# Router fed from x1, one route for the last four tiles, and a first expert's list built by one-hot matmuls

## The chip, the cores and the metric

The kernel runs on one core of a Trainium2 chip. The metric is the device time of one execution in microseconds, as the median of several runs. TensorE (PE) multiplies matrices, VectorE (DVE), ScalarE (ACT) and GpSimd (POOL) work on tiles of 128 partitions, SyncE (SP) issues most DMAs, and sixteen DMA engines move the data. The five engines run their own instruction streams in program order and wait for each other on semaphores.

## The reference

One layer of a mixer block on x of 2048 tokens by 1024 features (conditioning vector `c`), then a mixture of experts with 32 experts in 4 groups of 8. What bears on this change is its second half:

```python
mix = jnp.concatenate([y_conv, y_att, y_pool], axis=-1) @ w_out[l]
x = x + g1 * mix
h = _rmsnorm(x, norm2_g[l]) * (1 + sc2) + sh2
x = x + g2 * _hier_moe(h, ...)          # then a final rmsnorm
# in _hier_moe, per token (hf = h):
g_prob = softmax(hf @ rg_w + rg_b);           g_p, g_idx = top_k(g_prob, 1)
e_logits = einsum('td,dge->tge', hf, re_w) + re_b
e_sel = e_logits of group g_idx;              e_p, e_idx = top_k(softmax(e_sel), 2)
gates = g_p * e_p / sum(e_p)
y = (silu(hb @ w1[e]) * (hb @ w3[e])) @ w2[e]  # per expert e, hb = its tokens
out[token] += gate * y
```

Everything is float32. Each token goes to two experts of one group; expert weights are 1024 by 512 (w1, w3) and 512 by 1024 (w2).

## The kernel before

Convolution, projections and attention fill the span up to about 1144 us. The change lies in the two stages behind them.

**Output stage**, `output()` (L1087). It takes 16 tiles of 128 tokens. For a tile, `product` multiplies with w_out; `mm3` makes each float32 product of three passes on float32r parts (lines L92, L93, L94: high by high, low by high, high by low), so 48 matmuls of 512 columns. Then x1 = x + g1\*mix (L1132, L1133), a sum of squares on ACT (L1136), and h2 = x1\*s\*A2 + B2 on DVE (L1138, L1139), where s is 1/rms. h2 is written to memory (L1140, profile name h_d). `router` (L1142) transposes h2 on PE (L1152), copies it from PSUM on ACT (L1153), multiplies with the 36 router columns `rw` (L1157) and adds the bias (L1159). When a group of tiles (`GROUPS`: 4, 4, 4, 2, 2) has its logits, `route` (L1278) picks group and experts with a chain of small DVE instructions (L1269 to L1337), counts on PE how many earlier tokens each expert has (L1312 to L1318), and POOL scatters the entries (token, gate) into the experts' lists in memory, `list_d`, two indirect DMAs per tile (L1340). At the end `order` (L1344) ranks the experts by their counts into `ordi`.

**Experts**, `moe()` (L1420). The first two experts are fixed (`FIRST`), the other 30 come in the order of `ordi`, one SP register load each (L1451, TENSOR_LOAD). For an expert, SP reads its list (`gather`, L1573: `ent` from `list_d`), POOL gathers the tokens' rows (L1575: `xg` from `h_d`), PE transposes them (`flip`, L1603), and PE multiplies with the weights by `mm3`. The weights (`wr`, 512 KB or 1 MB loads, SP L1641) are cut into high parts on ACT (`wh`, L1657) and low parts on DVE or POOL (`wl`, L1658). Results are scattered back with L1708.

The order of instructions on every engine is set by a scheduler that works from estimated costs; the Python order and `issue_after` only bound it. An instruction that waits holds all behind it on its engine.

Of the kernel before, what the change touches and what calls it, by code (L numbers as in the profile page):

```python
# [10 lines left out]
F32 = mybir.dt.float32  # L11
# [3 lines left out]
I32 = mybir.dt.int32  # L15
AF = mybir.ActivationFunctionType
OP = mybir.AluOpType
# [4 lines left out]
T = 2048  # L22
D = 1024
# [24 lines left out]
class K:  # L48
# [1040 lines left out]
    def output(self):  # L1089
# [6 lines left out]
        with ExitStack() as c1:  # L1096
# [7 lines left out]
            with tc.issue_after(self.last.ins):  # L1104
# [5 lines left out]
                self.row(A2, 2)  # L1110
                rw = wp.tile([128, KT, 36], F32, name="rw")
# [4 lines left out]
                nc.sync.dma_start(rb[:, 4:36], a["router_e_b"].rearrange("o g e -> o (g e)").to_broadcast([128, 32]))  # L1116
            lgs = {}
            where = [(c, i) for c, n in enumerate(self.GROUPS) for i in range(n)]

            def product(t, mix):  # L1120
# [5 lines left out]
                for k in range(KT):  # L1126
                    for m in range(2):
                        s = slice(m * 512, (m + 1) * 512)
                        self.mm3(ps[:, m, :], mh[:, k, ti], ml[:, k, ti], W[k][0][:, s], W[k][1][:, s],
                                 k == 0, k == KT - 1)  # L1130
                h2 = st.tile([128, D], F32, name="h2", tag="h2", bufs=3)
                nc.vector.tensor_tensor(h2, ps.rearrange("p a b -> p (a b)"), g1, OP.mult)  # L1132
                nc.vector.tensor_tensor(x, x, h2, OP.add)  # L1133
                (nc.scalar if t == NT - 1 else nc.sync).dma_start(self.x1_d[t * 128:(t + 1) * 128], x)
                s = st.tile([128, 3], F32, name="s2", tag="s2", bufs=4)
                nc.scalar.activation(h2, x, AF.Square, accum_out=s[:, 0:1])  # L1136
                self.rsqrt(s[:, 2:3], s[:, 0:1], D, s[:, 1:2])
                nc.vector.scalar_tensor_tensor(h2, x, s[:, 2:3], A2, op0=OP.mult, op1=OP.mult)  # L1138
                nc.vector.tensor_tensor(h2, h2, B2, OP.add)  # L1139
                (nc.scalar if t == NT - 1 else nc.sync).dma_start(self.h2_d[t * 128:(t + 1) * 128], h2)  # L1140
                return h2

            def router(t, h2):
# [15 lines left out]
                nc.vector.tensor_tensor(lgs[c][:, i, :], pr[:, :36], rb, OP.add)  # L1159
# [67 lines left out]
    def route_consts(self, wp):  # L1227
# [31 lines left out]
        nc.vector.tensor_copy(self.capi, self.capr)  # L1259
# [566 lines left out]
```

## Time and profile before

| | |
|---|---|
| median of 3 runs | 2230.25 us (2230.12 to 2230.81) |
| profiled execution | 2232.48 us, of which the span 2230.6 us |
| PE busy in the span | 2008.2 us (90%) |
| DVE, ACT, POOL busy | 71%, 54%, 39% |
| DMA traffic | 569.64 MB, mean 255 GB/s |

In the profile, L numbers are lines of the kernel before; an arrow reads "output <- input". `big` and `sm` are PSUM tiles, `W` and `S`, `R`, `L` hold cut parts of w_out, `mh` and `ml` the high and low parts of the mixed input. A name in square brackets with a time is the idle time of the engine just before, and what ended it. PE is busy nearly without a break in the output stage and in most of the experts; between them, from 1362 to 1407 us, it is mostly idle.

### The profile page before, as it was taken

Reading aid. Unit: us, or ns where it says so; the run is one execution under the profiler, and the core shown is the slowest. Engines: PE = TensorE matmul, PEld = TensorE weight load, DVE = VectorE, ACT = ScalarE, POOL = GpSimd, SP = SyncE. Lnnn points to the kernel's source line nnn. Section 1 sums busy time; section 2 is a strip of 40 time slices with the busy share of each in tenths; the row PEclk is TensorE's granted clock in tenths of the full one; section 3 lists DMA queues with packets and bytes.
Section 4 is the critical chain, followed back from the end, with each engine's and each line's share of the span. In section 5 each row is a group of like instructions: output and inputs, shape, how many; then the busy total and the mean of one; then the engine's idle time right before and its main releaser. Section 6 shows DMA issues by size and latency. Waiting matters only on the chain. (4 is left out here: it accounts for less than half of the span.)

```text
span 2230.6 us, 37562 instructions
## 1 busy us (share of the span) xinstructions
PE 2008.2 (90%) x12823; PEld 1508.2 (68%) x12824; DVE 1578.8 (71%) x3007; ACT 1214.8 (54%) x2026; POOL 868.6 (39%) x1592
## 2 busy tenths in 40 slices
PE   5899999988889999988889995799999999999983
PEld 4777886855667777767767884557776666666762
DVE  5696899668878888886445555657766766766673
ACT  4832323256778887777642222546665665665552
POOL 4542112546454333365000113234544445554443
PEclk9999999998999999999999997899999999999987
DMA  8737978869977666668867436699999899999884
GB/s 283 259 120 231 277 219 278 292 188 295 293 236 224 200 206 197 206 190 276 225 220 277 152 124 224 237 291 358 336 316 319 279 347 319 338 326 313 304 297 141
DMA packets 312468, 569.64 MB, mean 255 GB/s; under 512 B 34547, under 2 KB 147656, under 8 KB 311240
## 3 DMA queue, kind: packets, MB, share of 16 engines
q1 hardware_dynamic: 287496, 489.26, 66.7%
q0 software_dynamic: 22304, 68.41, 10.7%
q10 hardware_dynamic: 2464, 9.44, 1.1%
q8 instruction: 105, 1.72, 0.3%
q14 instruction: 99, 0.81, 0.1%
HBM read 462.44 MB, written 103.53 MB: 254 GB/s over the span
## 5 line engine op out<-in xcount | busy, mean ns | idle before, releaser
L1658 DVE TENSOR_TENSOR wl<-wr,wh 128x1024 fp32r<-128x1024 f32 x314 | 393.1, 1289 | 173.0 <-ACT wh L1657 172.6
L1657 ACT ACTIVATE wh<-wr 128x1024 fp32r<-128x1024 f32 x372 | 374.2, 1053 | 243.7 <-PE acc L94 172.4
L93 PE MATMUL acc<-wl,xh 128*128 128x512 f32 (+3 forms) x544 | 219.4, 404 | 7.5 <-DVE wl L1658 3.9
L1026 DVE CUSTOM_DVE_ANT_0 L<-pl,bias 128x512 f32<-128x512 f32 (+3 forms) x312 | 180.3, 607 | 62.2 <-PE pt L1064 35.9
L92 PE MATMUL acc<-wh,xh 128*128 128x512 f32 (+3 forms) x544 | 217.0, 409 | 5.6 <-ACT wh L1657 5.2
L94 PE MATMUL acc<-wh,xl 128*128 128x512 f32 (+3 forms) x544 | 216.5, 401 | 0.0
L1025 PE MATMUL pl<-kc,qa 128*128 128x512 f32 (+3 forms) x640 | 183.6, 393 | 17.0 <-DMA kc<-kh_d 9.8
L863 DVE SCALAR_TENSOR_TENSOR S<-rel,wi,S 128x512 f32<-128x512 f32 (+3 forms) x259 | 171.2, 683 | 33.2 <-ACT rel L862 32.7
L1066 ACT ACTIVATE pT<-pt 128x512 f32<-128x512 f32 (+1 forms) x288 | 159.2, 577 | 63.9 <-PE pt L1064 62.9
L1064 PE MATMUL pt<-identr,L 128*128 128x128 f32 x1088 | 172.0, 284 | 20.5 <-ACT pT L1066 14.2
L1658 POOL TENSOR_TENSOR wl<-wr,wh 128x1024 fp32r<-128x1024 f32 x58 | 145.0, 2560 | 95.7 <-ACT wh L1657 92.5
L862 ACT ACTIVATE rel<-pi 128x512 f32<-128x512 f32 (+3 forms) x296 | 154.4, 549 | 48.1 <-PE pi L860 29.3
L627 DVE SCALAR_TENSOR_TENSOR ac<-u,kc,ac 128x512 f32<-128x512 f32 x240 | 175.0, 769 | 0.1
L1064 PEld LDWEIGHTS pt<-identr,L 128*128 128x128 f32 x1088 | 127.0, 143 | 61.6 <-ACT pT L1066 24.2
L1031 ACT ACTIVATE L<-L,ast 128x128 f32<-128x128 f32 (+15 forms) x128 | 154.1, 1205 | 17.1 <-DVE ast L1030 16.9
L1051 PE MATMUL po<-pT,vc 128*64 128x128 f32 x2176 | 150.5, 284 | 9.3 <-ACT pT L1066 9.0
L1051 PEld LDWEIGHTS po<-pT,vc 128*64 128x64 f32 x2176 | 123.5, 140 | 41.4 <-ACT pT L1066 20.3
L859 PE MATMUL pi<-kk,qi 128*128 128x512 f32 (+3 forms) x296 | 128.7, 437 | 23.3 <-ACT rel L862 22.9
L1025 PEld LDWEIGHTS pl<-kc,qa 128*128 128x128 f32 x640 | 108.9, 194 | 45.4 <-DVE ast L1026 16.4
L1708 POOL DMA_INDIRECT x_d<-yo,ent x32 | 93.6, 2926 | 97.1 <-DVE yo L1751 70.7
L92 PEld LDWEIGHTS acc<-wh,xh 128*128 128x128 f32 (+3 forms) x544 | 98.3, 183 | 42.7 <-ACT wh L1657 11.9
L93 PEld LDWEIGHTS acc<-wl,xh 128*128 128x128 f32 (+3 forms) x544 | 99.7, 183 | 39.6 <-DVE wl L1658 5.5
(525 smaller groups left out, 4615.8 us busy)
## 6 DMA issues: line engine op xcount, KB each, us to landing
wr<-in_exp_w_dram SPq DMA_DIRECT2D x256, 512.0 KB
wr<-in_exp_w_dram SPq DMA_DIRECT2D x64, 1024.0 KB
h<-h_d SPq DMA_DIRECT2D x64, 512.0 KB
vc<-v_d SPq DMA_DIRECT2D x112, 256.0 KB
h_d<-h POOLq DMA_DIRECT2D x32, 512.0 KB, 4.7
qa<-qa_d SPq DMA_DIRECT2D x128, 128.0 KB
modr<-in_mod_w_dram SPq DMA_DIRECT2D x32, 512.0 KB
xt<-in_x_dram SPq DMA_DIRECT2D x16, 512.0 KB
```

What stands on the lines that cost most here:

```text
L92: mm(out, lh, rh, start=start, stop=False)
L93: mm(out, lh, rl, start=False, stop=False)
L94: mm(out, ll, rh, start=False, stop=stop)
L627: nc.vector.scalar_tensor_tensor(acc[j], src, kc[:, j, i:i + 1], acc[j], op0=OP.mult, op1=OP.add)
L863: nc.vector.scalar_tensor_tensor(S[:, s:e], r[:, :e - s], self.wi[:, t, h:h + 1], S[:, s:e] if h else self.tie[:, s:e], op0=OP.mult, op1=O ...
L1025: nc.tensor.matmul(ps[:, :e - s], q[:, h % 2, m], k[:, s:e], start=m == 0, stop=m == 1)
L1026: nc.vector.tensor_tensor_reduce(L[:, s:e], ps[:, :e - s], bias[:, s:e], 1.0, -3e38, OP.add, OP.max, mx[:, i:i + 1])
L1051: nc.tensor.matmul(po[r], v[:, (k2 + i) % 4, r], pT[:, i, j], start=len(left) > 2 * t, stop=len(left) <= 2)
L1064: nc.tensor.transpose(pt[:, i, j], P[j][:, (k2 + i) * 128:(k2 + i + 1) * 128], self.ident)
L1066: nc.scalar.activation(pT[:, :m], pt[:, :m], AF.Copy)
L1657: nc.scalar.activation(H[:, s], W[:, s], AF.Copy)
L1658: (nc.gpsimd if pool else nc.vector).tensor_tensor(L[:, s], W[:, s], H[:, s].bitcast(F32), OP.subtract)
```

## The change

Five edits. (1) The router works on x1: since h2 = x1\*s\*A2 + B2, the logits are s\*(x1 @ (A2\*rw)) + (B2 @ rw + rb). A2\*rw is formed once, B2 @ rw by eight matmuls against a matrix of ones, for which A2 and B2 are loaded a second time as columns (`BA`). (2) The last tile makes its product one half of the columns after the other, with x1 and the squares by halves, and its h2 on ACT and POOL. (3) `GROUPS` becomes (4, 4, 4, 4). (4) Each route adds one-hot matmuls that collect the list of the first expert in `have`; after the last route it is turned into `en0`, so that this expert's rows are gathered without reading `list_d`. (5) The list scatters of the last route stand behind that gather.

```diff
                 self.row(A2, 2)
+                BA = wp.tile([128, 2, KT], F32, name="BA")
+                nc.sync.dma_start(BA, self.row_d[:, D:3 * D].rearrange("o (m k p) -> p (o m) k", m=2, k=KT))
                 rw = wp.tile([128, KT, 36], F32, name="rw")
...
+            full = wp.tile([128, 128], F32, name="full")
+            nc.vector.memset(full, 1.0)
+            rwB = wp.tile([128, KT, 36], F32, name="rwB")
+            nc.vector.tensor_tensor(rwB, rw, BA[:, 0, :, None].to_broadcast([128, KT, 36]), OP.mult)
+            nc.vector.tensor_tensor(rw, rw, BA[:, 1, :, None].to_broadcast([128, KT, 36]), OP.mult)
+            pb = self.sm()
+            for k in range(KT):
+                nc.tensor.matmul(pb[:, :36], full, rwB[:, k], start=k == 0, stop=k == KT - 1)
+            nc.vector.tensor_tensor(rb, rb, pb[:, :36], OP.add)
...
+                for m, k in ([(m, k) for m in range(2) for k in range(KT)] if last else
+                             [(m, k) for k in range(KT) for m in range(2)]):
...
+                if last:
                     for m in range(2):
...
+                        nc.vector.tensor_tensor(h2[:, f], ps[:, m], g1[:, f], OP.mult)
+                        nc.vector.tensor_tensor(x[:, f], x[:, f], h2[:, f], OP.add)
+                        nc.scalar.activation(h2[:, f], x[:, f], AF.Square, accum_out=s[:, 2 * m:2 * m + 1])
...
+                if last:
+                    nc.scalar.activation(h2, x, AF.Copy, scale=s[:, 3:4])
+                    for m in range(2):
+                        f = slice(m * 512, (m + 1) * 512)
+                        nc.gpsimd.tensor_tensor(h2[:, f], h2[:, f], A2[:, f], OP.mult)
+                        nc.gpsimd.tensor_tensor(h2[:, f], h2[:, f], B2[:, f], OP.add)
...
-                        nc.tensor.transpose(pt[:, k, :], h2[:, f:f + 128], self.ident)
+                        nc.tensor.transpose(pt[:, k, :], x[:, f:f + 128], self.ident)
...
-                nc.vector.tensor_tensor(lgs[c][:, i, :], pr[:, :36], rb, OP.add)
+                nc.vector.scalar_tensor_tensor(lgs[c][:, i, :], pr[:, :36], s, rb, op0=OP.mult, op1=OP.add)
...
-    GROUPS = (4, 4, 4, 2, 2)
+    GROUPS = (4, 4, 4, 4)
...
+        V.scalar_tensor_tensor(pos, ps[:, :, e:e + 1], 1.0, O[:, :, e:e + 1], op0=OP.add, op1=OP.mult)
+        M = st.tile([128, 4, 128], F32, name="slots", tag="slots", bufs=1)
+        for i in range(N):
+            V.tensor_scalar(M[:, i], self.slot1, pos[:, i], None, op0=OP.is_equal)
...
+        for i in range(N):
+            nc.tensor.matmul(pe[:, 0:3], M[:, i], self.ent[:, t0 + i], start=i == 0, stop=i == N - 1)
+        V.tensor_tensor(self.have, self.have, pe[:, 0:3], OP.add)
+        last = c == len(self.GROUPS) - 1
+        if last:
+            en0 = self.en0 = self.cst.tile([128, 2], I32, name="en0")
...
+            self.listed = V.tensor_copy(en0[:, 1:2].bitcast(F32), self.have[:, 1:2])
...
-        en = tile([2, 2], "en", I32)
+        en = self.cst.tile([128, 4, 2, 2], I32, name="enl") if last else tile([2, 2], "en", I32)
...
-        si = tile([2], "si", I32)
+        si = self.cst.tile([128, 4, 2], I32, name="sil") if last else tile([2], "si", I32)
         V.tensor_copy(si, sl)
-        for i in range(N):
+        if last:
+            self.late = en, si
+        else:
+            self.enter(en, si)
...
             prep(0)
+            with tc.issue_after(self.fetched.ins):
+                self.enter(*self.late)
             prep(1)
             self.moe_tiles()
-            self.flip(ex[0])
-            self.half1(0, ex[0])
+            with tc.issue_after(self.listed.ins):
+                self.flip(ex[0])
+                self.half1(0, ex[0])
```

`enter` is the old scatter loop over `en.shape[1]` tiles; `gather` takes `en0` in place of an `ent` read from `list_d`. L numbers in the order excerpts of the changed kernel are its own.

On PE, where the output stage begins, the order before goes from the last matmuls of the first tiles' earlier products straight on to the next ones (`big<-S,mh`):

```order
L94 MATMUL big<-W_21917,S 128x512
L92 MATMUL big<-W_21917,S 128x512
L93 MATMUL big<-W_21917,S 128x512
L94 MATMUL big<-W_21917,S 128x512
L92 MATMUL big<-S,mh 128x512 [waits DVE_49]
```

In the changed kernel the bias matmuls of `rwB`, and the transposes of an attention tile (`ol`), stand between:

```order
L94 MATMUL big<-W_21917,S 128x512
L1127 MATMUL sm<-rwB,full 128x36 [waits DVE_49]
L1127 MATMUL sm<-rwB,full 128x36 x7
L1234 MATMUL sm<-identr,ol 128x128 [waits DMAHW0_49]
L1234 MATMUL sm<-identr,ol 128x128 [waits DMAHW1_49]
L1234 MATMUL sm<-identr,ol 128x128 x6
L92 MATMUL big<-S,mh 128x512 [waits DVE_49]
```

What moved: PE reaches a wait for DVE's `rwB` before it may go on with the products.

On POOL, between the output stage and the experts, before (`s` is the 1/rms of a tile, `list_d` the lists, `xg` gathered rows; the last `list_d` rows are those of the fifth route):

```order
L1340 DMA list_d<-en,si 73728x2 [waits DMASW7_49,DVE_49]
L1340 DMA list_d<-en,si 73728x2 [waits DMASW0_49]
L1340 DMA list_d<-en,si 73728x2 [waits DMASW1_49]
L1340 DMA list_d<-en,si 73728x2 [waits DMASW2_49]
L1575 DMA xg<-h_d,ent 128x1024 [waits DMAHW3_49,DMAHW4_49,DMAHW2_49,DMAHW5_49,DMAHW1_49,DMAHW6_49,DMAHW0_49,DMAHW7_49,DMASW3_49,PE_49]
L1575 DMA xg<-h_d,ent 128x1024 [waits DMAHW4_49,DMAHW2_49,DMASW4_49]
```

and in the changed kernel (`enl`, `sil` are the last route's entries and slots; six more `list_d` rows follow the two shown, and then the second gather):

```order
L1163 TENSOR_TENSOR h_24153<-h_24153,A_21924 128x512
L1164 TENSOR_TENSOR h_24153<-h_24153,B_21922 128x512 [waits DMAHW3_49,Pool_49]
L1164 TENSOR_TENSOR h_24153<-h_24153,B_21922 128x512 [waits Pool_49]
L1646 DMA xg<-h_d,en_24346 128x1024 [waits DMAHW3_49,DMAHW2_49,DMAHW4_49,DMAHW1_49,DMAHW5_49,DMASW3_49,DMAHW7_49,DVE_49,PE_49]
L1406 DMA list_d<-enl,sil 73728x2 [waits DMASW4_49]
L1406 DMA list_d<-enl,sil 73728x2 [waits DMASW5_49]
```

What moved: the first gather stands ahead of the last route's scatters, which are now eight and not four, and the second gather (`xg<-h_d,ent`) behind all of them.

On SP, the list reads of the experts before (`ordi` rows are the register loads, ISA rows their address arithmetic):

```order
L1573 DMA ent<-list_d 128x2 [waits DMAHW3_49,DMASW2_49]
L1573 DMA ent<-list_d 128x2
L1451 TENSOR_LOAD ordi [waits DVE_49]
L1451 ISA x2
L1573 ISA
L1573 DMA ent<-list_d 128x2 [waits DMAHW5_49]
L1451 TENSOR_LOAD ordi
```

Of the remaining 28 register loads, one stands behind the next five weight loads, and the others one behind the other, ahead of any further weight load. In the changed kernel sixteen stand ahead of the first list read:

```order
L1517 TENSOR_LOAD ordi
L1517 ISA x2
L1644 DMA ent<-list_d 128x2 [waits DMAHW4_49,DMASW3_49]
L1644 ISA
L1644 DMA ent<-list_d 128x2
L1653 ISA
L1653 DMA enu<-list_d 64x2 [waits DMAHW6_49]
L1653 ISA
L1653 DMA enu<-list_d 64x2 [waits DMAHW7_49]
L1712 ISA
L1712 DMA wr<-in_exp_w_dram 128x2x512 [waits DMAHW0_49,DVE_49]
```

What moved: more than half of the register loads stand where SP waits for the scatters, and the other fourteen stand in groups of one to four between weight loads.

On PE, the transposes of the second expert's rows (`smm<-identr,xg`), which before stood behind the fourth matmul of the first expert, stand in the changed kernel here, behind 43 of them:

```order
L93 MATMUL acc<-wl,xh 128x512
L94 MATMUL acc<-wh,xl 128x512
L1674 MATMUL smm<-identr,xg 128x128 [waits DMASW4_49]
L1674 MATMUL smm<-identr,xg 128x128 x3
L1674 MATMUL smm<-identr,xg 128x128 [waits PE_49]
L1674 MATMUL smm<-identr,xg 128x128 x3
L93 MATMUL acc<-wl,xh 128x512 [waits DVE_49]
```

What moved: PE can do more of the first expert before it needs the second one's rows.

## Rows read from the trace of the kernel before

**Rows 1.** Windows: stretch, length, busy PE PEld DVE ACT POOL (counts), clock, DMA share, GB/s.

```profile
1200.00:1362.30 162.30, 162.30 (x1578) 130.48 (x1569) 91.33 (x204) 39.88 (x76) 31.92 (x35) 1.00 0.47 161
1362.30:1407.00 44.70, 8.85 (x212) 7.60 (x211) 26.86 (x105) 9.93 (x16) 17.40 (x13) 0.57 0.52 183
1415.00:1430.00 15.00, 14.90 (x73) 11.90 (x72) 13.45 (x13) 12.88 (x15) 2.40 (x3) 1.00 0.35 119
1458.00:1466.00 8.00, 4.50 (x10) 2.78 (x10) 8.00 (x7) 3.05 (x4) 5.97 (x3) 0.66 0.78 283
1466.00:1500.00 34.00, 33.57 (x156) 20.79 (x160) 17.05 (x20) 16.13 (x23) 8.87 (x7) 0.93 0.89 273
1500.00:2000.00 500.00, 494.93 (x2870) 340.74 (x2859) 352.41 (x368) 305.70 (x400) 252.87 (x122) 0.99 0.98 327
```

**Rows 2.** Timeline of PE: start, duration, line, operation, count, idle before and its releaser.

```profile
1361.93 0.40 PE L94 MATMUL big<-W,ml 128*128 128x512 f32 x1
1373.87 0.23 PE L1312 MATMUL sm<-O,tri 128*128 128x64 bf16 x1 [11.55 <-DVE O L1310]
...
1377.10 1.80 PE L1152 MATMUL sm<-identr,h 128*128 128x128 f32 x8
1378.84 1.60 PE L1157 MATMUL sm<-rw,hT 128*32 128x36 f32 x96
...
1406.97 1.26 PE L1603 MATMUL smm<-identr,xg 128*128 128x128 f32 x8 [18.04 <-DMA xg<-h_d,ent]
...
1411.28 1.18 PE L94 MATMUL acc<-wh,xl 128*128 128x512 f32 x2
...
1421.45 0.40 PE L93 MATMUL acc<-wl,xh 128*128 128x512 f32 x1
```

**Rows 3.** Timeline of DVE behind the last product.

```profile
1363.44 0.24 DVE L1334 COPY en<-tok 128x2 int32<-128x2 int32 x2 [8.28 <-DMA list_d<-en,si]
...
1380.49 0.20 DVE L1159 TENSOR_TENSOR lg<-sm,rb 128x36 f32<-128x36 f32 x1 [0.92 <-PE sm L1157]
...
1384.82 0.23 DVE L1310 TENSOR_TENSOR O<-oe 128x64 bf16<-128x64 f32 x1
...
1387.79 0.15 DVE L1337 CAST si<-sl 128x4 int32<-128x4 f32 x1
...
1389.66 6.88 DVE L1658 TENSOR_TENSOR wl<-wr,wh 128x1024 fp32r<-128x1024 f32 x6
```

**Rows 4.** Timeline of POOL: the last route's scatters, the first gather.

```profile
1389.47 0.96 POOL L1340 DMA_INDIRECT list_d<-en,si  x1 [0.30 <-issue]
1390.73 6.64 POOL L1340 DMA_INDIRECT list_d<-en,si  x1 [0.31 <-issue]
...
1402.67 0.98 POOL L1575 DMA_INDIRECT xg<-h_d,ent  x1 [4.04 <-DMA ent<-list_d]
```

**Rows 5.** The page's groups of instructions: POOL's low parts (busy, mean ns).

```profile
L1658 POOL TENSOR_TENSOR wl<-wr,wh 128x1024 fp32r<-128x1024 f32 x58 | 145.0, 2560 | 95.7 <-ACT wh L1657 92.5
```

**Rows 6.** Timeline of SP between output stage and experts.

```profile
1399.83 2.02 SPq L1573 DMA_DIRECT2D ent<-list_d  x3
...
1429.00 13.11 SPq L1641 DMA_DIRECT2D wr<-in_exp_w_dram  x11
```

**Rows 7.** Line 1451, the register loads: durations min/median/max in ns, first and last start.

```profile
L1451 SPq TENSOR_LOAD <-ordi x30: 261/266/294, 1400.7 to 1427.8; - x30
```

**Rows 8.** Timeline of SP where the output stage begins.

```profile
1164.45 3.86 SPq L1113 DMA_DIRECT2D rw<-in_router_e_w_dram  x1
1168.35 3.76 SPq L1115 DMA_DIRECT2D rb<-in_router_g_b_dram  x1
```

**Rows 9.** Timeline of PE at the start of the output stage's products.

```profile
1175.10 0.50 PE L92 MATMUL big<-S,mh 128*128 128x512 f32 x1 [0.18 <-DVE h L1132]
```

**Rows 10.** Window behind the idle stretch before the output stage, columns as in rows 1.

```profile
1147.90:1153.20 5.30, 5.29 (x13) 4.14 (x14) 2.67 (x16) 2.36 (x3) 0.73 (x6) 0.50 0.62 210
```

**Rows 11.** Timeline of DVE in the first route, the row behind the counts from PE.

```profile
1233.64 0.29 DVE L1328 TENSOR_TENSOR q<-sm,slot 128x128 f32<-128x128 f32 x1 [0.51 <-PE sm L1314]
```

More of the change, by code (lines that the diff above doesn't have):

```diff
@@ L1133, in product @@
[L1133 to L1139, printed above, removed]
@@ L1140, in product @@
-                (nc.scalar if t == NT - 1 else nc.sync).dma_start(self.h2_d[t * 128:(t + 1) * 128], h2)
-                return h2
-            def router(t, h2):
+                last = t == NT - 1
+                for m, k in ([(m, k) for m in range(2) for k in range(KT)] if last else
+                             [(m, k) for k in range(KT) for m in range(2)]):
+                    s = slice(m * 512, (m + 1) * 512)
+                    self.mm3(ps[:, m, :], mh[:, k, ti], ml[:, k, ti], W[k][0][:, s], W[k][1][:, s],
+                             k == 0, k == KT - 1)
@@ L1144, in router @@
+                (nc.scalar if last else nc.sync).dma_start(self.h2_d[t * 128:(t + 1) * 128], h2)
+                return x, s[:, 3:4]
+            def router(t, x1):
+                x, s = x1
                 c, i = where[t]
@@ L1335, in route, with enter @@
         V.tensor_copy(en[:, :, :, 1].bitcast(F32), g)
-        si = tile([2], "si", I32)
+        si = self.cst.tile([128, 4, 2], I32, name="sil") if last else tile([2], "si", I32)
         V.tensor_copy(si, sl)
-        for i in range(N):
+        if last:
+            self.late = en, si
+        else:
+            self.enter(en, si)
+    def enter(self, en, si):
+        nc = self.nc
+        for i in range(en.shape[1]):
             for j in range(2):
@@ L1446, in prep @@
                 if i < 2:
-                    self.gather(ex[i], FIRST[i], 128, 0)
+                    self.gather(ex[i], FIRST[i], 128, 0, self.en0 if not i else None)
                 elif i < 32:
@@ L1562, in load2, with gather @@
         return [self.load([x["w"][2][:, 2 * c:2 * c + 2]]) for c in range(2)]
-    def gather(self, x, e, N, first):
+    def gather(self, x, e, N, first, en0=None):
         nc, mp = self.nc, self.mp
@@ L1570, in gather @@
         for o, nb in bs:
-            en = (self.cst.tile([128, 2], I32, name=f"ent{o}") if x.get("last") else
-                  mp.tile([128, 2], I32, name="ent", tag="ent", bufs=12))
-            nc.sync.dma_start(en[:nb], lst[bass.ds(e, 1), bass.ds(first + o, nb), :].rearrange("e s w -> (e s) w"))
+            en = en0 if en0 is not None else (
+                self.cst.tile([128, 2], I32, name=f"ent{o}") if x.get("last") else
+                mp.tile([128, 2], I32, name="ent", tag="ent", bufs=12))
+            if en0 is None:
+                nc.sync.dma_start(en[:nb], lst[bass.ds(e, 1), bass.ds(first + o, nb), :].rearrange("e s w -> (e s) w"))
             xg = mp.tile([128, D], F32R, name="xg", tag="xg", bufs=4)
-            nc.gpsimd.indirect_dma_start(out=xg[:nb].bitcast(F32), out_offset=None, in_=self.h2_d,
+            self.fetched = nc.gpsimd.indirect_dma_start(out=xg[:nb].bitcast(F32), out_offset=None, in_=self.h2_d,
                                          in_offset=bass.IndirectOffsetOnAxis(ap=en[:nb, 0:1], axis=0))
```

35 lines of the change are left out of this document (29 added, 6 removed).

## The prediction

> **What bounds the kernel now.** I read the windows first, then the timelines of the engines around the seam of output stage and experts. In the output stage PE has no idle microsecond, at full clock, with the DMA engines half used [rows 1]: there the order on PE alone counts, and what is put into it is paid. The last product matmul ends at 1361.93 + 0.40 = 1362.3; I call that moment T0 and count the seam from it. From T0 to 1407 PE is busy 8.85 of 44.7 us [rows 1]. The first cause is a wait on DVE: at 1363.44 it takes up a copy into `en` for which it had waited 8.28 us, until the third route's scatters had read that buffer [rows 3]; everything of the last two tiles stands behind it, and PE's next row comes 11.55 us after the last product [rows 2]. Then run the last route (logits 1380.49, choice 1384.82, slots 1387.79 [rows 3]), its scatters, SP's list read at 1399.83 [rows 6], the gather at 1402.67 [rows 4] and PE's transposes at 1406.97, behind 18.04 us of idle [rows 2]. Of the scatters one takes 6.64 us and not 0.96 [rows 4]: it ends at 1397.37, just behind the six cuts that DVE runs from 1389.66 to 1396.54 [rows 3].
>
> Behind the seam comes a second, weaker bound. From 1415 to 1430 the DMA engines are busy 0.35 [rows 1], while SP works through register loads; 30 of these, 0.27 us each beside their address arithmetic, the last at 1427.8 [rows 7], and the next weight loads go out at 1429.00 [rows 6]. PE feels it later: at 1458 to 1466 it is busy 4.50 of 8 us at clock 0.66, and up to 1500 the clock is 0.93 [rows 1]. Afterwards PE is busy 494.93 of 500 us with DMA at 0.98 [rows 1], so time won at the seam is kept as long as the weights come that much earlier too.
>
> **The change part by part.** *Bias from x1, start of the stage.* `BA` is 2 x 8 single floats on each of 128 partitions, 2048 pieces of four bytes, put ahead of the router weights on SP. Before, the load of `rw`'s expert part, 1024 pieces, and the load behind it hold SP 3.86 and 3.76 us, until 1172.1 [rows 8]. PE meets its wait for `rwB` where it now starts the next products at 1175.10 [rows 9]. `rwB` needs `BA` and the whole `rw`. If 2048 more pieces hold the queue as two loads of 1024 do at most, that is 7.6 us; if they go along with the others, almost nothing. With `rw` landing at about 1172 before, that gives 1172 to 1180, plus a multiplication on DVE (128x288, about 0.5 by the 0.29 of a 128x128 one [rows 11]); PE's stall lies between 0 and 6.5 us, and I take 4, since the two rows nearest in kind both show the hold. [...] Together 5.5, between 0 and 9.1.
>
> [...]
>
> *One-hot matmuls in routes 0 to 2.* On PE they stand directly behind the counts on which DVE's `pos` and `slots` wait. Before, DVE answers 0.51 us after PE's counts and then works 0.29 on one 128x128 operation [rows 11]. Now PE waits for `pos`, `q` and the first slots: about 0.7 us in two routes, and 2.0 in the third, where a 128x1024 operation of the h2 chain lies between on DVE, 1.15 or a little more by the cuts [rows 3]. Twelve small float32 matmuls add about 0.5 us per route. Together 4.7, between 1.5 (the matmuls alone) and 7. All of it is in the stage without idle time, so it moves T0. Slip of T0: 5.5 + 4.7 = 10.2.
>
> *The wait for `en` goes,* since the last route writes into a tile of its own. What is late next is the real chain. The halves buy nothing: in the changed order DVE's multiply of the first half waits for PE and that of the second has no wait of its own, so both start at the product's end. With T0 the new end of the products: four half operations of about 0.65 (a 128x1024 cut takes 6.88/6 = 1.15 [rows 3]) to T0+2.6; transposes, copies and router matmuls as from 1377.10 to the logits at 1380.69, 3.6 us [rows 2, 3], with half a microsecond overlapped, T0+5.6; choice as 1380.49 to 1385.05, 4.6, T0+10.2; slots 2.9 as before [rows 3] and about 1.2 for the added `pos`, `slots` and `ga`, T0+14.3; `en0` T0+15.2. Beside it POOL's four half operations, 1.28 each from 2.56 for a whole one [rows 5], end at about T0+11, and h2's write, if it takes the 4.3 us of a gather at most, lands by about T0+15: hidden, by a hair. The gather goes at T0+15.2, PE has rows 4.3 us later (1402.67 to 1406.97 [rows 2, 4]), T0+19.5. The low-by-high pass needs DVE's `xl`, which stands behind `order`'s small steps and the six cuts: T0+17.7 + 6.9 + 1.3, so the first L94 at about T0+26.3. Before it was at 1411.28 [rows 2], T0+49.0. The first expert starts 22.7 us earlier, counted from T0.
>
> *The second expert.* Its gather now stands behind eight scatters, not four, and these behind the first gather. Eight cost 8 x 1.26 = 10.1 us [rows 4] from T0+16.4. I take it that they are held by DVE's cuts as in the row of 6.64 us: the first six cuts, and after `xl` the cuts of the next weights; with about 11 us of holding they end at T0+37.4. List read at T0+38.6, gather 2.8 later as before (1399.83 to 1402.67 [rows 4, 6]), rows 4.3 after that: T0+45.9, transposes to T0+47.3. PE has 43 matmuls before that and is through at about T0+36; it then waits about 10 us and goes on at the lower clock, 1.3 us. Matmul 44 is at T0+48.6, before at 1421.45 [rows 2], T0+59.1: 10.5 won. With the slip of 10.2 that is about 0 at this point.
>
> *Register loads.* Sixteen now stand where SP waits for the scatters, fourteen in groups between weight loads. The hole of 1415 to 1430 goes: 15 x 0.65 = 10 us of DMA time [rows 1], less the later start of the stream, which stands behind the list read: T0+38.6 with the slip is 1411, against 1399.83 [rows 6]. What it can give PE is what PE loses between 1458 and 1500: 3.5 idle + 4.50 x 0.34 = 1.5 + 0.4 + 33.57 x 0.07 = 2.4, together 7.8 [rows 1]. I take 6, between 0 and 7.8.
>
> *The rest* (scatter count of the routes, one route fewer, h2 of the last tile on ACT and POOL, constants) is hidden behind PE in the stage or lies in the chain above.
>
> Sum: +10.2 - 10.5 - 6 = -6.3. Against the profiled execution, 2232.48, that is 2226.2; the profiled one lies 2.2 above the median of the runs, so I forecast 2230.25 - 6.3 = 2224 us, own range 2218 to 2230.
>
> **The rivals.** (A) *The scatters are not held.* For it: the scatter of 1389.47 took 0.96 although the first cut began 0.19 behind its start [rows 3, 4]. Against: the next one, with its 6.64. Then they end at T0+26.5, the second expert's rows are there at T0+35 and PE does not wait: matmul 44 at T0+35.5, 13 us earlier than in the forecast; part of it is lost again to weights that do not come as fast, so 9 of it: 2215. [...]
>
> (B) *All is paid back in the stage.* The `BA` stall with its clock at 9.1 and routes of 5.5 to 7 move T0 by 15 to 16 us, so PE is 5 late at matmul 44, and the weights' 6 are used up: 2229. For it: both rows behind the 1024 pieces show a hold of 3.8 us [rows 8]. Against: DMA engines serve the pieces beside other traffic.
>
> (C) *Slower: the second expert's gather starves.* DVE runs cuts nearly without a break once weights land (13.45 of 15 us [rows 1]). If the eight scatters get through only behind the twelfth cut, at T0+34, they end at T0+44, the rows come at T0+52.6 and matmul 44 at T0+55: only 4 won, and weights that wait behind the list read start 7 us later still, so the hole is merely moved. With a slip of 10 to 15: 6 to 11 slower, 2238. It decides when the scatters end later than about T0+42. Against: two scatters should be through before the first cut.
>
> (D) *The change doesn't do what it says*, for instance the first gather waits for more than `en0` and h2. Its row waits for several DMA queues; if one of these is the six weight loads that now go out as h2 is done, the first expert begins about 8 us later, but PE still waits at the second: close to the forecast, 2226.
>
> **How the numbers follow.** A difference under 0.2% (4.5 us) can't be told from no change. Forecast with D: 0.47; A: 0.16; B: 0.19; C: 0.18. Faster by over 0.2% (below 2225.8): all of A and about two thirds of the forecast's own range, 0.48. Slower (above 2234.7): C and a little of B, 0.20. The rest 0.32 within. The range takes in most of A and C: 2212 to 2238.
>
> **What would show it.** After the change PE should show, near 1175, an idle of 2 to 6 us ended by DVE's `rwB`, and a clock of 0.5 behind it; small idles ended by `slots` in three routes; T0 near 1372. No `en` wait on DVE. The first gather at T0+15, the first L94 at T0+26, a PE idle of about 10 us ended by the second gather's DMA at T0+46, and scatters with one or two rows of several microseconds. No DMA hole behind 1415. The forecast is wrong if T0 moves by less than 5 or more than 14, if the second gather is not what PE waits for, or if PE's losses at 1458 to 1500 stay although the hole is gone.

## The result, and the profile after

| | before | after |
|---|---|---|
| median, same chip | 2230.12 us (9 runs) | 2215.47 us (9 runs, 2206.29 to 2222.8) |
| ratio, 95% interval | | 0.9938 [0.9922, 0.9954] |
| profiled execution, its span | 2232.48, 2230.6 us | 2222.8, 2220.7 us |

The kernel became faster by 14.7 us. The forecast was 2224, with a range of 2212 to 2238. Time and direction are as forecast; the reasons are not, as the experiments show. (2215 is the number of rival A, whose mechanism did not come, and lies below the 2218 to 2230 of the main line.) The seam first, by windows of the kernel after (columns as in [rows 1]):

```profile
1200.00:1362.30 162.30, 159.16 (x1498) 129.37 (x1497) 93.28 (x227) 37.49 (x71) 30.95 (x36) 0.98 0.38 131
1366.90:1407.00 40.10, 20.05 (x244) 16.33 (x242) 26.76 (x81) 15.26 (x23) 20.74 (x14) 0.66 0.69 256
1415.00:1430.00 15.00, 11.86 (x51) 9.48 (x51) 7.86 (x9) 7.46 (x9) 1.66 (x2) 0.73 0.99 375
1458.00:1466.00 8.00, 7.01 (x38) 3.68 (x38) 7.70 (x10) 5.95 (x8) 1.59 (x1) 1.00 1.05 393
1466.00:1500.00 34.00, 34.00 (x195) 21.27 (x192) 17.60 (x19) 15.75 (x22) 12.20 (x8) 1.00 0.92 296
1500.00:2000.00 500.00, 494.16 (x2839) 339.60 (x2837) 352.10 (x366) 308.00 (x405) 263.67 (x123) 1.00 0.97 326
```

The output stage, without an idle microsecond before, has lost 3.1 us of PE. The DMA hole of 1415 to 1430 is gone (0.35 to 0.99), and so are nearly all losses of 1458 to 1500 (1.0 us is left of the 7.8). Between T0 (now 1366.52 + 0.39 = 1366.9) and 1407 PE works twice as long as before. Its timeline around the seam, to be held against [rows 2]:

```profile
1366.52 0.39 PE L94 MATMUL big<-W,ml 128*128 128x512 f32 x1
...
1380.23 0.29 PE L1349 MATMUL sm<-O,tri 128*128 128x128 bf16 x1 [8.49 <-DVE O L1347]
...
1395.96 1.25 PE L1674 MATMUL smm<-identr,xg 128*128 128x128 f32 x8 [8.27 <-DMA xg<-h_d,en]
...
1399.26 1.05 PE L94 MATMUL acc<-wh,xl 128*128 128x512 f32 x2
...
1417.61 1.25 PE L1674 MATMUL smm<-identr,xg 128*128 128x128 f32 x8 [7.61 <-DMA xg<-h_d,ent]
1418.66 0.76 PE L93 MATMUL acc<-wl,xh 128*128 128x512 f32 x1
```

The choice is made at T0+13.3 (the start of PE's counts, `sm<-O,tri`; so in all that follows; before at T0+22.8), the first expert begins at T0+29.1, its first L94 stands at T0+32.4, and the second gather's rows come at T0+50.7. The wait that was forecast last is last, 4.8 us late. POOL's timeline shows why:

```profile
1372.62 2.50 POOL L1163 TENSOR_TENSOR h<-h,A 128x512 f32<-128x512 f32 x2 [1.26 <-DMA wr<-in_exp_w_dram]
1375.08 2.53 POOL L1164 TENSOR_TENSOR h<-h,B 128x512 f32<-128x512 f32 x2
1388.32 1.05 POOL L1646 DMA_INDIRECT xg<-h_d,en  x1 [10.72 <-DVE ov L1448]
1389.68 6.50 POOL L1406 DMA_INDIRECT list_d<-enl,sil  x1 [0.30 <-issue]
1396.48 0.97 POOL L1406 DMA_INDIRECT list_d<-enl,sil  x1 [0.30 <-issue]
...
1409.65 1.94 POOL L1646 DMA_INDIRECT xg<-h_d,ent  x1 [3.68 <-DMA ent<-list_d]
```

and DVE's beside it:

```profile
1373.01 0.91 DVE L1310 TENSOR_TENSOR fo<-fo,fk 128x16 f32<-128x16 f32 x1
...
1373.96 1.31 DVE L1334 TENSOR_TENSOR te<-lg,fo 128x128 f32<-128x128 f32 x1
...
1376.47 1.18 DVE L1308 TENSOR_TENSOR fo<-fo,dec 128x32 f32<-128x32 f32 x1
...
1377.91 0.19 DVE L1310 TENSOR_TENSOR fo<-fo,fk 128x32 f32<-128x32 f32 x1
...
1388.41 6.88 DVE L1729 TENSOR_TENSOR wl<-wr,wh 128x1024 fp32r<-128x1024 f32 x6
```

While POOL forms h2, until 1377.61, three of DVE's small steps of the choice take 0.91, 1.31 and 1.18 us; once POOL is done the same line takes 0.19. In defer_h2_on_dve, where POOL has no part in the last tile's h2, the small steps take 0.17 to 0.29; by what means POOL's work lengthens them no run shows. And h2, ready at 1377.61, is written late, as ACT's timeline tells:

```profile
1382.57 0.36 ACTq L1168 DMA_DIRECT2D h_d<-h  x1
1382.98 5.79 ACT L1728 ACTIVATE wh<-wr 128x1024 fp32r<-128x1024 f32 x6 [3.81 <-DMA wr<-in_exp_w_dram]
```

The write goes out 5.0 us after h2 is there, and the gather, whose entries `en0` are ready at 1386.28, at 1388.32: T0+21.4, not T0+15.2.

### The profile page after: what moved, and what is told of

The parts are those of the page before. It is cut to its first block, busy times and chain, and to the rows that moved or that the text cites. A ratio compares the mean times of both kernels' runs of the same rounds, so it can differ in the third digit from the quotient of the medians.

```text
span 2220.7 us, 37647 instructions
## 1 busy us (share of the span) xinstructions
PE 2008.4 (90%) x12857; PEld 1512.5 (68%) x12858; DVE 1573.5 (71%) x3016; ACT 1215.7 (55%) x2027; POOL 885.2 (40%) x1599
## 2 busy tenths in 40 slices
DMA packets 314388, 569.65 MB, mean 257 GB/s; under 512 B 36467, under 2 KB 149576, under 8 KB 313160
## 3 DMA queue, kind: packets, MB, share of 16 engines
q1 hardware_dynamic: 289560, 489.79, 65.8%
## 5 line engine op out<-in xcount | busy, mean ns | idle before, releaser
L1729 DVE TENSOR_TENSOR wl<-wr,wh 128x1024 fp32r<-128x1024 f32 x314 | 388.0, 1274 | 157.6 <-ACT wh L1728 156.5
L1026 DVE CUSTOM_DVE_ANT_0 L<-pl,bias 128x512 f32<-128x512 f32 (+3 forms) x312 | 180.5, 608 | 57.7 <-PE pt L1064 32.3
L94 PE MATMUL acc<-wh,xl 128*128 128x512 f32 (+3 forms) x544 | 215.7, 400 | 0.0
L862 ACT ACTIVATE rel<-pi 128x512 f32<-128x512 f32 (+3 forms) x296 | 154.2, 548 | 47.5 <-PE pi L860 28.5
L1064 PEld LDWEIGHTS pt<-identr,L 128*128 128x128 f32 x1088 | 126.0, 143 | 61.1 <-ACT pT L1066 22.6
L859 PE MATMUL pi<-kk,qi 128*128 128x512 f32 (+3 forms) x296 | 128.5, 436 | 23.3 <-ACT rel L862 22.8
```

The source lines that it names most:

```text
L94: mm(out, ll, rh, start=False, stop=stop)
L1026: nc.vector.tensor_tensor_reduce(L[:, s:e], ps[:, :e - s], bias[:, s:e], 1.0, -3e38, OP.add, OP.max, mx[:, i:i + 1])
L1064: nc.tensor.transpose(pt[:, i, j], P[j][:, (k2 + i) * 128:(k2 + i + 1) * 128], self.ident)
L1729: (nc.gpsimd if pool else nc.vector).tensor_tensor(L[:, s], W[:, s], H[:, s].bitcast(F32), OP.subtract)
```

## The experiments

Fourteen profiled executions are compared by four marks: when attention ends (start of PE's last transposes of its output `oT`), from there to T0, from T0 to the first transposes of the first expert's hidden values (`hr`; the expectations call it matmul 72), and from there to the end of the span. Place 1 is where the tiles of attention and of the w_out parts begin, modulo 256 bytes; place 2 where `mh` and `ml` begin, modulo 64. No trace shows an address: the places follow from the order and the sizes of the tiles.

| kernel | place 1; 2 | attention ends | to T0 | to `hr` | to the end | ratio to before |
|---|---|---|---|---|---|---|
| before | 128; 32 | 1143.1 | 219.2 | 65.8 | 802.4 | |
| before_again | 128; 32 | 1149.0 | 219.0 | 66.2 | 799.4 | |
| place_early_only | 0; 32 | 1134.7 | 218.8 | 65.5 | 801.2 | 0.9933 |
| place_late_only | 128; 0 | 1148.9 | 215.8 | 66.9 | 796.9 | 0.9981 |
| before_shifted | 0; 0 | 1135.2 | 215.6 | 66.5 | 798.8 | 0.9958 |
| own_entries_shifted | 0; 0 | 1132.7 | 214.9 | 68.4 | 800.7 | 0.9948 |
| after | 0; 0 | 1136.7 | 230.2 | 60.5 | 793.2 | 0.9938 |
| same_again | 0; 0 | 1137.7 | 237.2 | 59.4 | 792.3 | 0.9972 |
| after_misplaced | 64; 0 | 1141.0 | 233.7 | 59.8 | 793.2 | 1.0014 |
| defer_onehot | 0; 0 | 1130.8 | 220.8 | 59.8 | 791.0 | 0.9909 |
| defer_h2_on_dve | 0; 0 | 1138.0 | 220.9 | 62.1 | 789.5 | 0.9923 |
| own_queue_for_h2 | 0; 0 | 1135.8 | 221.0 | 57.7 | 793.7 | 0.9890 |
| two_lists | 32; 0 | 1145.0 | 230.7 | 49.7 | 797.7 | 0.9965 |
| two_lists_in_place | 0; 0 | 1140.1 | 225.9 | 47.5 | 796.1 | 0.9870 |

**The two kernels again** (`same_again`, `before_again`, no edit), because attention, which the change does not touch, ended 6.4 us earlier.

> The changed kernel once more, unchanged, for a second trace of it. The profile after gained 9.9 us of span on the profile before, and 6.4 of these lie ahead of the change: the last attention transposes start at 1137.0 and not 1143.4, in the same instruction order. Theory 1 (the attention stage wanders from execution to execution): here its end lies anywhere between 1136 and 1145, and the time from there to the end of the span (1083.6 in the first trace of after, 1087.1 before) repeats within 4 us or shows one stall more or less at the weights. Theory 2 (something of the change makes attention faster): its end is again at 1137 within 1 us. Median by either about 2215.

> The kernel before once more, unchanged, for a second trace of it. Theory 1: the end of attention (last transposes of oT, 1143.4 in the first trace) moves by several us, also below 1140. Theory 2: it is again at 1143 to 1144, so that the changed kernel really has the shorter attention stage.

Measured: 2227.39 us, 0.9972 [0.9958, 0.9985] (12 runs), and 2235.49 in one run. The gain of this kernel is 0.3 to 0.6%, and its two intervals do not overlap, so between ratios that were taken on different chips a difference of 0.3% is no result. In `same_again` T0 is 7.0 us later than in the execution above, 1.4 of them ahead of the products; the rest are stalls in the small router matmuls that nothing in the trace releases ("issue"), and the lower clock behind them (0.62 from 1353 to 1362):

```profile
1353.06 0.26 PE L1186 MATMUL sm<-rw,hT 128*32 128x36 f32 x4 [0.99 <-issue]
...
1355.91 0.22 PE L1186 MATMUL sm<-rw,hT 128*32 128x36 f32 x1 [1.16 <-issue]
```

**Place alone.** The change's new tiles among the constants (`en0`, `enl`, `sil`) take 128 bytes and move all that is laid behind them; the tiles of the output stage move `mh` and `ml` too. So: the kernel before, its instructions and their order untouched, with unused tiles.

```diff
         self.capi = self.cst.tile([1, 32], I32, name="capi")
+        self.cst.tile([128, 32], I32, name="pad")   # before_shifted, place_early_only
+        wp.tile([128, 8], I32, name="padow")        # before_shifted, place_late_only
```

> The kernel before with two unused tiles of 128 and 32 bytes per partition: no instruction is added and the order is the same on all engines; every later tile of the on-chip memory lies 128 bytes higher (the attention, expert weight and w_out tiles, as in the changed kernel, whose own new constants shift them by the same 128), and mh, xr and h of the output stage start at a multiple of 64 bytes, which before they did not. Layout theory (the changed kernel is faster ahead of the change only because its tiles lie elsewhere): the last attention transposes start at 1131 to 1139 as in three traces of that layout (1136.7, 1137.7, 1130.8), not at 1143 to 1149; the 13th attention tile takes 21 to 23 us and not 25; the products of the output stage come every 0.2295 us and not 0.2335, 3 us over the stage; the time falls by 7 to 12 us without any edit of the change. Chance theory: attention ends at 1141 to 1150, the spacing stays 0.2335, and the time is within 2 us of before.

> The kernel before, its instructions and their order untouched, with one unused tile of 128 bytes among the constants, so that all tiles behind it lie 128 bytes further on (the tiles of attention and of the output weights at a multiple of 256, those of the output stage's operands still at 32 beyond a multiple of 64). Theory (place decides, by two separate means): attention ends early, at 1130 to 1138 us and not at 1143 to 1149, but a product matmul keeps its 0.2335 us, so the output stage still takes 219 from the last attention transposes to the last product; time about 2222 to 2225. Rival 1 (only the operands of the output stage count, the attention's end varies by itself): 2228 to 2231. Rival 2 (the two go together): as before_shifted, 2220.

> The kernel before, its instructions and their order untouched, with one unused tile of 32 bytes among the output stage's constants, so that the operands of the output stage's products begin at a multiple of 64 bytes and nothing ahead of them moves. Theory: attention ends as before, 1143 to 1149, a product matmul takes 0.2277 instead of 0.2335 us, and the output stage is 3.5 us shorter; time about 2225 to 2227. Rival 1 (attention's place alone counts): 2229 to 2231. Rival 2 (the two go together): as before_shifted, 2220.

Measured: 2220.02 us, 0.9958 [0.9942, 0.9975]; 2219.71, 0.9933 [0.9908, 0.9958]; 2229.47, 0.9981 [0.9966, 0.9996]. With no work changed, an unused tile of 128 bytes gives what the whole change gave. The places together, in before_shifted, gave no more than the first alone; on two chips that is not resolved. In the traces two effects are apart. Attention ends at 1130.8 to 1140.1 (mean 1135.7) in the nine executions with place 1 at a multiple of 256, and at 1141.0 to 1149.0 (mean 1145.4) in the five without. It is a stage of loads: windows of 470 to 640, of place_late_only and then of place_early_only,

```profile
470.00:640.00 170.00, 143.82 (x1079) 96.25 (x1079) 135.01 (x359) 117.84 (x255) 85.90 (x315) 0.97 0.91 268
```

```profile
470.00:640.00 170.00, 150.50 (x1140) 101.34 (x1140) 140.68 (x372) 122.41 (x266) 87.13 (x315) 0.98 0.90 283
```

DMA engines that are as busy (0.91, 0.90) move 268 and 283 GB/s; in this window the five show 268 to 277, the nine 280 to 285. The places of the five lie 32, 64 and 128 bytes beyond a multiple of 256; by what means the place counts for these loads no run here shows. The second effect stands in PE's rows: starts of product matmuls in place_early_only, twelve apart, and in place_late_only, six apart:

```profile
1250.16 0.39 PE L93 MATMUL big<-L,mh 128*128 128x512 f32 x1
...
1252.95 0.40 PE L93 MATMUL big<-L,mh 128*128 128x512 f32 x1
```

```profile
1251.62 0.40 PE L93 MATMUL big<-L,mh 128*128 128x512 f32 x1
...
1252.99 0.39 PE L93 MATMUL big<-L,mh 128*128 128x512 f32 x1
```

Over 1200 to 1330 a product matmul takes 0.2333 us from start to start with `mh` at 32 beyond a multiple of 64, and 0.2280 at a multiple of 64; over 768 matmuls that is 4.1 us, and the stage is 3.2 shorter (219.0 to 215.8 in the table).

**The change without its place** (`after_misplaced`), the same code with one more unused tile of 64 bytes.

```diff
         self.capi = self.cst.tile([1, 32], I32, name="capi")
+        self.cst.tile([128, 16], I32, name="pad")
```

> The changed kernel with an unused tile of 64 bytes per partition ahead of its late constants: same order on all engines, tiles 64 bytes higher, so that those of attention and weights no longer start at multiples of 128 bytes. Layout theory: attention ends later than in after, at 1141 to 1150, and the time is 4 to 10 us above that of after. If only the start at a multiple of 64 bytes counts, it stays at 1137 and the time within 3 us; chance theory likewise.

Measured: 2232.44 us, 1.0014 [1.0, 1.0027]. Out of its place the change is worth nothing; place_late_only, which lies off 256 and at a multiple of 64 as well, gave 0.9981 without the change, though on another chip.

**The wait for `en`** (`own_entries_shifted`): the kernel before, laid as before_shifted, with the last route's entries in tiles of their own.

```diff
-        en = tile([2, 2], "en", I32)
+        en = self.cst.tile([128, 2, 2, 2], I32, name="enl") if last else tile([2, 2], "en", I32)
-        si = tile([2], "si", I32)
+        si = self.cst.tile([128, 2, 2], I32, name="sil") if last else tile([2], "si", I32)
```

> The kernel before in the same shifted layout, and of the change one part alone: the last route's entries and slots (en, si) in tiles of their own. If the wait of 8.28 us on VectorE at the end of the products is worth what the prediction says, VectorE's h of the last tile starts within 1 us of the last product, the choice of the last route's experts lies 5 to 8 us nearer to the last product than before (22.5), and the first expert's first matmul at 39 to 41 us behind the last product and not 46.1. Against before_shifted 5 to 7 us faster; if the weights bound the experts anyway, less than 2 us.

Measured: 2218.95 us, 0.9948 [0.9933, 0.9962], as before_shifted. The choice comes at T0+24.0, in before_shifted at T0+24.1. But before_shifted does not have the wait that this edit takes away. Of five executions with the order of the kernel before, `before` alone shows it; in before_again, the same kernel, DVE copies into `en` without idle time ahead of it:

```profile
1361.73 1.23 DVE L1132 TENSOR_TENSOR h<-big,g 128x1024 f32<-128x1024 f32 x1 [8.52 <-PE big L94]
1362.99 1.23 DVE L1133 TENSOR_TENSOR xr<-xr,h 128x1024 f32<-128x1024 f32 x1
1364.14 0.23 DVE L1334 COPY en<-tok 128x2 int32<-128x2 int32 x2
```

DVE's idle stands further ahead there, put down to a product of PE that had ended by 1358.3; what it waits for is not shown. It takes up the last tile at T0+2.3 to T0+4.1 in the four others and in own_entries_shifted, at T0+6.7 in `before`. The row of own_entries_shifted, at T0+4.1:

```profile
1351.67 1.22 DVE L1132 TENSOR_TENSOR h<-big,g 128x1024 f32<-128x1024 f32 x1
```

What these five gain is lost again on PE: in the router matmuls of the last tile they show five to seven idles that nothing in the trace releases, 2.7 to 3.2 us in all, and `before` shows none. In before_again the longest is

```profile
1385.75 0.50 PE L1157 MATMUL sm<-rw,hT 128*32 128x36 f32 x17 [1.15 <-issue]
```

So the choice comes at T0+22.6 to T0+24.3 with the wait and without it. Why the router matmuls stall stays open.

**One-hot matmuls later** (`defer_onehot`): those of routes 0 to 2 are issued behind a later tile's product.

```diff
+                if t > 4 and t % 4 == 2:
+                    with tc.issue_after(self.mm.ins):
+                        self.collect()
...
+        def collect():
+            pe = self.sm()
...
```

> The one-hot matmuls of routes 0 to 2 are put behind the next products but one, where the slots are long there; nothing else differs. In the trace of after, PE stands idle 0.65, about 0.7 and 1.84 us before them in the three routes. If these waits (and the lower clock behind the longest) are what the one-hot matmuls cost, the end of the last product counted from the end of attention goes from 229.8 to 225 or 226, and the time falls by 3 to 5 us. If the cost is the matmuls themselves (8 rows of about 0.1 us and their weight loads per route), it stays above 228 and the time within 2 us.

Measured: 2212.13 us, 0.9909 [0.9891, 0.9927]. In the kernel after, PE shows the waits that the prediction named, and one that is smaller:

```profile
1167.74 1.98 PE L1127 MATMUL sm<-rwB,full 128*128 128x36 f32 x16 [0.42 <-DVE rwB L1123]
...
1230.23 0.38 PE L1376 MATMUL sm<-entc,slots 128*128 128x3 f32 x2 [0.65 <-DVE slots L1370]
...
1285.23 0.38 PE L1376 MATMUL sm<-entc,slots 128*128 128x3 f32 x2 [0.65 <-DVE slots L1370]
...
1340.28 0.38 PE L1376 MATMUL sm<-entc,slots 128*128 128x3 f32 x2 [1.84 <-DVE slots L1370]
```

The third costs more than its 1.84 us. Windows of the kernel after and then of defer_onehot:

```profile
1338.00:1350.00 12.00, 10.16 (x80) 8.52 (x78) 5.75 (x16) 2.28 (x4) 4.72 (x6) 0.72 0.34 106
```

```profile
1338.00:1350.00 12.00, 12.00 (x123) 9.99 (x122) 4.55 (x6) 2.23 (x4) 5.74 (x7) 1.00 0.34 113
```

Behind it the granted clock falls, 0.72 over these 12 us (0.51 from 1344 to 1348). Deferred, no route waits, the clock stays, and the stage is 9.4 us shorter.

**h2 of the last tile on DVE** (`defer_h2_on_dve`: the edit above, and lines L1138 and L1139 of before for the last tile too, the write still ACT's).

```diff
-                if last:
-                    nc.scalar.activation(h2, x, AF.Copy, scale=s[:, 3:4])
...
+                nc.vector.scalar_tensor_tensor(h2, x, s[:, 3:4], A2, op0=OP.mult, op1=OP.mult)
+                nc.vector.tensor_tensor(h2, h2, B2, OP.add)
```

> defer_onehot with the last tile's h2 on VectorE as before, not on ScalarE and GpSimd. In the trace of after, VectorE's small steps of the last route take 0.91, 1.31 and 1.18 us while GpSimd's four h2 operations run (1372.6 to 1377.6), where they take 0.17 to 0.29 behind them, so the choice comes at 13.1 us behind the last product and not 10. If GpSimd holds VectorE there, these steps all take under 0.4 us now; two operations of 1.28 and 1.22 us stand between them instead, so the choice comes at 11.5 to 13 us, h2's write goes out before it, the first gather by 20 and not 21.4 us; time 0 to 2 us faster than defer_onehot. If they were slow for another reason, the long steps stay.

Measured: 2213.24 us, 0.9923 [0.9907, 0.9938], no gain. DVE's small steps are short again (0.17 to 0.29), but another wait took the place. ACT, and below it DVE:

```profile
1371.25 0.36 ACTq L1161 DMA_DIRECT2D h_d<-h  x1
1371.67 0.22 ACT L1324 ACTIVATE ex<-ex 128x16 f32<-128x16 f32 x1 [8.43 <-DMA wr<-in_exp_w_dram]
```

```profile
1371.92 0.17 DVE L1326 TENSOR_REDUCE gp<-ex 128x4 f32<-128x16 f32 x1 [5.23 <-ACT ex L1324]
```

ACT's write waits until a weight load (`wr`) has landed, and the exponentials of the choice stand behind it: the choice is at T0+17.2.

**h2 by POOL's queue** (`own_queue_for_h2`).

```diff
-                (nc.scalar if last else nc.sync).dma_start(self.h2_d[t * 128:(t + 1) * 128], h2)
+                (nc.gpsimd if last else nc.sync).dma_start(self.h2_d[t * 128:(t + 1) * 128], h2)
```

> As defer_h2_on_dve, with the last tile's h2 written by POOL's queue directly ahead of the first gather, not by ACT's. Theory (ACT's exponentials stood 5.2 us behind a write that waited for a weight load on the same queue): the choice is made at T0+11 to 12 and not at T0+17, the first gather goes at T0+18 to 19, PE is at the first expert's matmuls at T0+28 and at the third's transposes (matmul 72) at T0+57 to 59, against 62.1; time 2 to 4 us under defer_h2_on_dve's, about 2209 to 2211. Rival (the scatters' end sets the second expert's rows, whenever the first gather goes): matmul 72 stays at T0+60 to 62 and the time at 2212 to 2214.

Measured: 2209.44 us, 0.9890 [0.9867, 0.9912]. The choice is at T0+12.0. POOL:

```profile
1364.43 0.63 POOL L1161 DMA_DIRECT2D h_d<-h  x1 [3.16 <-DMA h_d<-h]
1375.65 1.04 POOL L1646 DMA_INDIRECT xg<-h_d,en  x1 [10.59 <-DMA wr<-in_exp_w_dram]
1376.99 7.76 POOL L1406 DMA_INDIRECT list_d<-enl,sil  x1 [0.30 <-issue]
```

The gather goes at T0+18.8, 0.8 us behind its entries. The scatter behind it takes 7.76 us and ends 0.9 after the sixth of DVE's cuts, as in the kernel after and in [rows 3, 4]; PE then waits 8.95 us for the second expert.

**Both fixed experts' lists** (`two_lists`: defer_onehot, with the one-hot list for the second expert too; `two_lists_in_place`: the same on own_queue_for_h2, both lists in one tile and 32 bytes of padding, so that the places are those of the kernel after).

```diff
-        e = FIRST[0]
+        for f, e in enumerate(FIRST):
...
-                    self.gather(ex[i], FIRST[i], 128, 0, self.en0 if not i else None)
+                    self.gather(ex[i], FIRST[i], 128, 0, self.en0[:, i])
```

> As the one before, and the second fixed expert's list is built by one-hot matmuls too, so that both first gathers stand ahead of the last route's scatters. Seam theory (PE waits at the 44th matmul for the second expert's rows, which wait for scatters and list read): the idle of 7.6 us before the second expert's transposes goes, with about 2 us of low clock behind it; the second rows are there by 10 us behind the first matmul; against defer_onehot 7 to 10 us faster, less 1 to 2 for 16 more small matmuls and the added small steps of VectorE ahead of the first gather. Rival (the weights are the bound there, so PE would wait for them instead): within 3 us of defer_onehot, with the idle now ended by high or low parts of the weights between 1410 and 1440.

> As own_queue_for_h2, with the second fixed expert's list by one-hot matmuls too, so that neither of the first two gathers stands behind the scatters; the added tiles are laid so that attention and the products have the same places modulo 256 and 64 bytes as in the changed kernel. Theory (the scatters' end is the last wait of the seam): PE's wait for the second gather goes, matmul 72 comes at T0+46 to 50, and the twelve more small matmuls, issued late, cost 1 to 3 us of the output stage; time about 2202 to 2207, the fastest of all. Rival (the stream of expert weights then sets the pace, whatever the seam gives): new waits on weights or on DVE's cuts between matmul 72 and the eighth expert, end at most 3 us earlier than own_queue_for_h2.

Measured: 2225.64 us, 0.9965 [0.9952, 0.9979], and 2204.85, 0.9870 [0.9845, 0.9894]. In the first, w_out's parts lie at 32 beyond a multiple of 64, a matmul takes 0.2335 us and attention ends at 1145.0. In place it is the fastest kernel of all by its median, though its interval overlaps own_queue_for_h2's. PE there:

```profile
1235.04 0.50 PE L94 MATMUL big<-L,ml 128*128 128x512 f32 x1 [0.85 <-DVE ml L88]
...
1392.17 1.26 PE L1688 MATMUL smm<-identr,xg 128*128 128x128 f32 x8 [4.39 <-DMA xg<-h_d,en]
...
1415.92 0.85 PE L1688 MATMUL smm<-identr,xg 128*128 128x128 f32 x8 [1.89 <-DMA xg<-h_d,ent]
```

The second fixed expert's transposes no longer wait; the wait of 1.89 is a later one. The seam wins 10.2 us (57.7 to 47.5). The stage pays 4.9 (0.85, 0.89 and 0.91 us for `ml` in three routes, and the matmuls), and 2.4 are lost later, so what is won at the seam is not all kept.

## Why the prediction was right, and where it was not

The time fell into the range, and the sign was right, but that is luck: the largest term of the gain is not in the sum. At equal place, after and same_again against before_shifted and own_entries_shifted, the means of the marks give: to T0 +18.5, to `hr` -7.5, later -7.0, together +4 where the sum said -6.3; the measured ratios (0.9938 and 0.9972 against 0.9958 and 0.9948) say no difference. The gain is the place of the tiles, a step that the prediction did not have: "constants" stood among what is hidden. By its own sign the forecast fails as well: less than 5 or more than 14 us for T0 was to show it wrong, and T0 moved by 4.6 from the span's start, because attention ended 6.4 earlier, and by 14.6 at equal place (after against before_shifted). The two other signs held: PE waits for the second gather, and nearly all losses of 1458 to 1500 are gone.

- *Bias from x1, 5.5.* Of this, 4 were the stall and 1.5 a lower clock behind it, a figure that no run shows; the runs show in its place an idle of 0.42 us and, at clock 0.60 and 0.55, a loss of 1.6. The hold on SP was right, its sum was not. `rw` is held 7.43 us behind `BA`, against 7.6, but not on top of the 3.86 and 3.76 of [rows 8]: the two loads behind it now take 0.58 each.

```profile
1156.31 0.38 SPq L1112 DMA_DIRECT2D BA<-row_d  x1
1157.01 7.43 SPq L1114 DMA_DIRECT2D rw<-in_router_g_w_dram  x1
1164.48 0.58 SPq L1115 DMA_DIRECT2D rw<-in_router_e_w_dram  x1
1165.10 0.58 SPq L1117 DMA_DIRECT2D rb<-in_router_g_b_dram  x1
```

The `rb` row ends 29.0 us behind attention's end, as before, and PE waited 0.42 us for `rwB`, not 4. Why one hold replaces the others, no run shows. Until the products' start the stage lost 1.6 us at equal place (33.5 against 31.9 from attention's end). The lower clock behind it (0.60 and 0.55 from 1170 to 1174) cost as much again: the first router matmuls come 13.2 us behind the products' start, in same_again and defer_onehot 11.6. Together 3.2.

- *One-hot routes, 4.7.* The mechanism was right, idles of 0.65, 0.65 and 1.84 against 0.7, 0.7 and 2.0. The size was not. From the products' start to T0 it is 196.7 us, deferred 187.5; of these 9.2, 1.6 are the bias's clock, and 7.6 the waits of the routes with the clock behind them. A further 3.8 (187.5 against 183.7 in before_shifted) are the matmuls and slower products. The clock behind an idle stretch was counted for `BA`, not here; and the 0.5 us a route for the matmuls themselves, given without a row, are 0.8 in defer_onehot (1235.09 to 1235.89).
- *The wait for `en`, first cause.* Wrong, and read from a single execution: in four others of the same order the wait is not there, and the choice comes no earlier. What shortens it from T0+22.8 to T0+13.3 should be the one route and the router from x1; these two, and the halves, were not tried apart.
- *h2 "hidden, by a hair".* Wrong twice: beside POOL's work three steps of DVE's choice take 0.91 to 1.31 us, and the write goes out on ACT's queue 5.0 us after h2 is there. Gather at T0+21.4 and not T0+15.2. Rival D was near this, and its "close to the forecast" held.
- *Scatters and second gather.* Held, as forecast, but by about 6.5 us and not 11, and begun 6.4 later: they end at T0+39.1 against T0+37.4. The gathered rows reach PE 8.0 us behind the gather's start, not 4.3. Matmul 44 is at T0+51.8 against T0+48.6, so the seam won 7.3 there, not 10.5. The 1.3 us for a lower clock behind that wait no run shows; the runs show a clock of 0.50 from 1417.6 to 1421, behind 7.61 us of idle. Rival A falls: a single scatter took 6.50, 7.76 and 6.87 us beside six cuts (after, own_queue_for_h2, two_lists_in_place). In all fourteen executions the scatter that runs beside the six cuts ends 0.8 to 0.9 us behind the last of them (0.83 in `before`, 0.89 in after, 0.90 in own_queue_for_h2, 0.85 in two_lists_in_place); no run took the cuts away.
- *Register loads, 6.* From `hr` to the end all six executions with the one list need 789.5 to 793.7 us, the six without the change 796.9 to 802.4, 7.7 less by the means. The hole is gone with it; it was not undone alone, and the part behind `hr` is not free of the seam (two_lists_in_place comes to `hr` earlier and takes 796.1).
- *Rival B,* all paid back in the stage, is what happened to the edits themselves, a slip of 15 and more at equal place, though by the routes and not by `BA`. What stood against it held: from 1157.0 to 1164.5, while SP was held behind `BA`, the DMA engines moved 349 GB/s (320 in `before` from 1164.45 to 1172.11). *Rival C* did not come: the scatters end at T0+39.1, and it began at T0+42.

## What to carry to other kernels

Before a small gain is put down to an edit, pad the old kernel to the new one's addresses: here 128 unused bytes gave as much as the edit (0.9933 and 0.9938). Before a wait is called the cause, take a second trace of the same kernel: 8.28 us of idle stood in one of five. In a stage where one engine has no idle time, put new work behind something already waiting to run, never directly behind the result that it needs: here the stalls were 0.65, 0.65 and 1.84 us, the clock behind the last fell to 0.51, and the stage was 9.4 us shorter without them. Ahead of a chain that sets the end, put no DMA with a wait on the engine that the chain uses: behind ACT's write in defer_h2_on_dve DVE waited 5.23 us for the exponentials.

## What the runs showed of the hardware

- Tiles loaded by DMA at a multiple of 256 bytes (nine executions): attention ended 9.7 us earlier by the means, at equal work, than with tiles 32, 64 or 128 bytes beyond one (five).
- PE's products started every 0.2333 to 0.2335 us on average where either operand lies at 32 beyond a multiple of 64, and every 0.2270 to 0.2301 where both are at a multiple. The experts' matmuls (1500 to 2000) started every 0.2316 us in own_queue_for_h2 and every 0.2299 in two_lists_in_place: what sets it there is open.
- An indirect DMA issued on POOL beside unbroken cuts on DVE ended 0.8 to 0.9 us after the last cut in all fourteen executions, whichever of the scatters it was; the six scatters behind it in after took 0.96 to 0.97 each.
- Behind a load of 2048 pieces of four bytes the next issue on SP took 7.43 us, and the next two 0.58 each; without that load these two took 3.86 and 3.76. The page of after counts 36467 DMA packets under 512 B, that of `before` 34547.
- Runs of 36-column matmuls stalled on PE with no releaser in the trace: 2.7 to 3.2 us of idle in five executions at the last tile (the longest in before_again 1.15), none in another of the same order.
